# A hybrid mLSTM and gated DeltaNet layer on one core: a small tile is folded into another, and the mixers' tiles are padded

## The chip, the core and the metric

The kernel runs on one core of a Trainium2 chip. A core has five engines that work side by side: TensorE for matmuls (PE in the profile, with its weight loads as PEld), VectorE (DVE), ScalarE (ACT), GpSimd (POOL) and SyncE (SP), which here only issues transfers. They share an on-chip memory of 128 partitions (SBUF). A tile's place in it is a byte offset that is the same in all partitions, and "address" below means this offset. Matmuls accumulate in PSUM. The metric is the time of one execution on the device in microseconds (us). Before the change three runs gave a median of 2145.65 us, from 2143.23 to 2148.91.

## What is computed

One decoder block on 512 rows of width 2048, in float32. A single projection of the normalised input feeds an mLSTM branch with 8 heads and a gated DeltaNet branch with 16 heads; both go through one output projection and are merged with gates. Cut to what matters:

```python
u = rmsnorm(x, norm_w)                        # 512 x 2048
proj = u @ w_in                               # 2048 x 20528 columns
(ml_q, ml_k, ml_v, ml_o, ml_z, ml_i, ml_f,
 dn_qkv, dn_z, dn_b, dn_a, gate_a, gate_b) = split(proj)
h_a = mlstm_chunkwise(ml_q, ml_k, ml_v, softcap(ml_i), log_sigmoid(softcap(ml_f)))
h_a = rmsnorm_per_head(h_a) * ml_norm_w * sigmoid(ml_o) * silu(ml_z)
dq, dk, dv = split(silu(causal_conv(dn_qkv)))
g = -exp(a_log) * softplus(dn_a + dt_bias)    # log decay
h_b = gated_delta_chunkwise(l2norm(dq), l2norm(dk), dv, sigmoid(dn_b), g)
h_b = rmsnorm_per_head(h_b) * dn_norm_w * silu(dn_z)
y = sigmoid(gate_a) * (h_a @ w_out[:2048]) + sigmoid(gate_b) * (h_b @ w_out[2048:])
out = rmsnorm(x + y, final_norm_w)
```

## The kernel before

**The split of numbers.** A float32 weight is split in two pieces, `wh` (by ScalarE, `split_hi`, L146) and `wl` (the rest, by VectorE, `split_lo`, L149), and so are the activations, `uh` and `ul`. Each product is three matmuls: high by high, high by low, low by high. The matmuls' operands of 512 columns stream past a 128x128 block that was loaded before.

**The stages, in time.** First a front block, to 113.55 us: the normalisation, the transposes of the input, the first projections (`proj_cm`, L279) and the gates (`gates`, L460). Then the *seven-product stage* on `w_in`, to 1199.75 us. It computes two column blocks of 512 at a time with seven products of blocks in place of eight (`seven_stage`, L554). Its 14 pairs are listed in `SEVEN` (L52); each pair has 16 quads (8 of kind A, 8 of kind B), a quad of kind A has four products and one of kind B three, and a product (`product`, L646) is two rows of three matmuls, L652 to L654. That makes 14 x 56 x 6 matmuls, all of 512 columns. Then the *mixers*, which alternate the remaining projections (L272 to L274, L290 and L292) with the small matmuls of the two recurrences (`dn_back`, L1195, `dn_chain`, L1254, and the mLSTM heads behind them), among them groups of 128 and of 257 columns. Behind them come wide blocks on `w_out` (L1598 to L1600), the same seven-product function on `w_out` to about 2092 us, a last block and a short tail.

**Pieces in the seven-product stage.** For each quad SyncE loads three blocks of weights into a tile `wr3`. VectorE forms sums of them (`first_sums`, L590; the pair of sums is the tile `t13`). `split` (L581) then makes the pieces: *narrow* ones of 512 columns from the pool `wp` (tags `wh`, `wl`), and *wide* ones that hold two operands of 512 columns, from the stage's pool (tags `w2h`, `w2l`; each has two buffers of 4096 bytes). In a quad of kind A the products use the pieces in the order narrow, narrow, wide, wide; in kind B wide, wide, narrow. The order at a block's end (L675) puts the last two quads' narrow products together. In the profile a wide and a narrow low piece are both called `wl`.

**Where the tiles stand.** A pool places its tiles one behind the other in the order of their first use. The pool `sbp` (L422) of the first seven-product stage holds the tiles below; `turns` is declared 16 columns wide and one is used: +1 in the first 64 partitions, -1 in the others. `decay` (L888) uses it as a scale, beside a bias column of `pgam` with the negated decays, for heads `n` that are odd; so in `pgam`, with its 16 columns per chunk, the even columns are never read.

| tile | bytes | start |
|---|---|---|
| `w2h` | 2 x 4096 | 74752 |
| `pgam` | 256 | 82944 |
| `turns` | 64 | 83200 |
| `wr3` | 3 x 6144 | 83264 |
| `t13` | 4096 | 101696 |
| `w2l` | 2 x 4096 | 105792 |

The other operands of this stage's matmuls, the narrow pieces, `uh`, `ul`, `suh`, `sul`, `s4h` and `s4l`, start at multiples of 512. The final seven-product stage has a pool of its own (`sb2`) without `pgam` and `turns`; there `w2l` stands at 103424 and 107520.

**What sets the order.** TensorE's order is that of the code. On the other engines a scheduler orders instructions by readiness and priority: `high_priority` and `urgent(level)` (L225) lift an instruction, and `behind` (L152) puts it right behind the newest split. The mixers' generators are advanced by `tick` (L239) between groups of matmuls, so their small matmuls stand in fixed places among the projections.

Of the kernel before, what the change touches and what calls it, by code (L numbers as in the profile page):

```python
# [8 lines left out]
F32 = mybir.dt.float32  # L9
# [6 lines left out]
P = 128  # L16
S = 512
NC = S // P
D = 2048
KT = D // P  # L20
NB = 256
# [39 lines left out]
def hybrid_body(  # L61
# [18 lines left out]
    V, A, G, T = nc.vector, nc.scalar, nc.gpsimd, nc.tensor  # L80
# [144 lines left out]
    def urgent(level=1):  # L225
        return tc.high_priority(offset=level * PRIO)
# [195 lines left out]
    sbp = sbs.enter_context(tc.tile_pool(name="sbp", bufs=1))  # L422
# [31 lines left out]
    beta = cp.tile([P, NC, DNH], F32, tag="beta", name="beta")  # L454

    pgam = sbp.tile([P, NC, DNH], F32, tag="pgam", name="pgam")
    turns = sbp.tile([P, 16], F32, tag="turns", name="turns")[:, 0:1]
    for a, sign in ((0, 1.0), (64, -1.0)):
        G.memset(turns[a:a + 64], sign)
    def gates():  # L460
        rows = [sbp.tile([P, 3, S], F32, tag="wr3", name="grow", bufs=3) for _ in range(3)]

# [12 lines left out]
        tb = sml[:, 0, :, 0:16]  # L475
# [70 lines left out]
        A.activation(negeg, pc[:, :, 16:32], AF.Exp)  # L546
        V.tensor_copy(pgam[64:P], pc[64:P, :, 16:32])
        V.tensor_scalar(out=pgam[0:64], in0=pc[0:64, :, 16:32], scalar1=-1.0, scalar2=None, op0=ALU.mult)
        V.tensor_scalar(out=ngam, in0=pc[:, :, 16:32], scalar1=-1.0, scalar2=None, op0=ALU.mult)
        V.tensor_scalar(out=negeg, in0=negeg, scalar1=-1.0, scalar2=None, op0=ALU.mult)  # L550
        V.tensor_copy(acol, pc[:, :, 0:8])
# [447 lines left out]
    wk = wks.enter_context(tc.tile_pool(name="wkp", bufs=2))  # L999
    wkb = wkbs.enter_context(tc.tile_pool(name="wkb", bufs=2, side="right"))  # L1000
# [1 line left out]
    NYP = 2  # L1002
    yps = []
    for i in range(NYP):
        t = wkb.tile([P, S + 3], F32, tag=f"yp{i}", name=f"yp{i}", bufs=1)
        G.memset(t[:, 0:3], 0.0)
        yps.append(t)
    tb = wk.tile([P, 2 * NC, P], F32, tag="tb", name="tb", bufs=1)
    G.memset(tb, 0.0)
    ta = wk.tile([64, 2 * NC, 64], F32, tag="ta", name="ta", bufs=1)  # L1010
# [163 lines left out]
    def dn_front_q(hs, kq, u):  # L1174
        for j in range(2):
            pk = psw.tile([P, NC, P], F32, tag="wk", name="pqk")
            for c in range(NC):
                tsl = slice(c * P, (c + 1) * P)
                T.matmul(pk[:, c, :], kq[j][:, 0, tsl], kq[j][:, 1, tsl], start=True, stop=True)  # L1179
            dm, eg, ge = u["dm"][j]  # L1180
            with urgent():
                V.tensor_tensor(out=u["aq"][j][:, :, 1, :], in0=pk, in1=dm, op=ALU.mult)
            qt = kq[j][:, 1, :].rearrange("p (c t) -> p c t", t=P)
            G.tensor_tensor(out=qt, in0=qt, in1=eg, op=ALU.mult)
            u["qt"].append(qt)
            yield 1
        yield 9
        qe = wk.tile([P, 2, NC], F32, tag="qe", name="qe")
        with behind("A"):
            for j in range(2):  # L1190
                token_norms(u["qn"][j], qe[:, j, :])
        V.tensor_scalar(out=qe, in0=qe, scalar1=EPS, scalar2=EPS * P, op0=ALU.add, op1=ALU.mult)
        u["qe"] = qe

    def dn_back(hs, kq, u):  # L1195

        tn, tt = u["tn"], u["tt"]
        G2 = [(j * NC + c, u["aq"][j][:, c, 0, :]) for j in range(2) for c in range(NC)]
        for b in range(4):
            bs = slice(b * BS, (b + 1) * BS)  # L1200
            G.tensor_copy(tb[bs, :, bs], tt[bs])
        for b in range(2):
            bs = slice(b * BS, (b + 1) * BS)
            G.tensor_copy(ta[bs, :, bs], tn[bs])
        p1 = psw.tile([P, 2 * NC, BS], F32, tag="wk", name="p1")
        for g, a in G2:
            for q in range(2):
                a0, a1 = slice(64 * q, 64 * q + 32), slice(64 * q + 32, 64 * q + 64)
                T.matmul(p1[a1, g, :], a[a0, a1], tn[a0, g, :], start=True, stop=True)
        s1 = wk.tile([P, 2 * NC, BS], F32, tag="s3", name="s1", bufs=1)  # L1210
        for q in range(2):
            a1 = slice(64 * q + 32, 64 * q + 64)
            with urgent():
                A.mul(s1[a1], p1[a1], -1.0)
        for j in range(2):
            vn = u["vs"][j]
            with behind("V"):
                V.tensor_tensor(out=vn, in0=vn, in1=bc(u["nk"][:, j, :], P), op=ALU.mult)
        yield 2
        p2 = psw.tile([P, 2, 2 * NC, BS], F32, tag="wk", name="p2")  # L1220
        for g, a in G2:
            for q in range(2):
                a0, a1 = slice(64 * q, 64 * q + 32), slice(64 * q + 32, 64 * q + 64)
                T.matmul(p2[a0, 0, g, :], s1[a1, g, :], tt[a1, g, :], start=True, stop=True)
            T.matmul(p2[32:64, 1, g, :], tt[32:64, g, :], s1[32:64, g, :], start=True, stop=True)
        with urgent(2):
            V.tensor_copy(ta[32:64, :, 0:32], p2[32:64, 1])
        for q in range(2):
            a0, a1 = slice(64 * q, 64 * q + 32), slice(64 * q + 32, 64 * q + 64)
            with urgent():  # L1230
                A.copy(tb[a0, :, a1], p2[a0, 0])
        yield 3
        p3 = psw.tile([P, NC, 64], F32, tag="wk", name="p3")
        for c in range(NC):
            T.matmul(p3[64:128, c, :], G2[c][1][0:64, 64:128], ta[:, c, :], start=True, stop=True)
            T.matmul(p3[0:64, c, :], G2[NC + c][1][64:128, 0:64], tb[64:128, NC + c, 64:128], start=True, stop=True)
        s3 = wk.tile([P, NC, 64], F32, tag="s3", name="s3", bufs=1)
        with urgent():
            A.mul(s3[64:128], p3[64:128], -1.0)
            V.tensor_tensor(out=s3[0:64], in0=p3[0:64], in1=u["cs"][0:64, 1, :].unsqueeze(2).to_broadcast([64, NC, 64]),  # L1240
                            op=ALU.mult)
        yield 3
        p4 = psw.tile([P, NC, 64], F32, tag="wk", name="p4")
        for c in range(NC):
            T.matmul(p4[0:64, c, :], s3[64:128, c, :], tb[64:128, c, 64:128], start=True, stop=True)
            T.matmul(p4[64:128, c, :], ta[:, NC + c, :], s3[0:64, c, :], start=True, stop=True)
        with urgent():
            V.tensor_copy(tb[0:64, 0:NC, 64:128], p4[0:64])
            A.mul(tb[0:64, NC:2 * NC, 64:128], p4[64:128], -1.0)
        soon = hs[0] == 2 * UNITS[-1]  # L1250
        start(dn_chain(0, hs, kq, u, soon), 3 - soon)
        start(dn_chain(1, hs, kq, u, soon), 4 - soon)

    def dn_chain(j, hs, kq, u, soon):  # L1254
# [2 lines left out]
        vn = u["vs"][j]  # L1257

        po = pso.tile([P, NC, P], F32, tag="o", name="po")
        ssq = wk.tile([P, NC], F32, tag="ssq", name="ssq")  # L1260
        st = None
        for c in range(NC):
            tsl = slice(c * P, (c + 1) * P)
# [98 lines left out]
    def ml_head(h):  # L1362
# [25 lines left out]
        qi = qT.rearrange("p (c t) -> p c t", t=P)  # L1388
        G.tensor_tensor(out=qi, in0=qi, in1=iwb, op=ALU.mult)
        yield 3  # L1390
        v1 = wkb.tile([P, NC, NB + 16], F32, tag="mv1", name="v1", bufs=1)[:, :, 0:NB + 1]
        G.memset(v1[:, :, NB:NB + 1], 1.0)
        nc.sync.dma_start(v1[:, :, 0:NB], v_d[:, :, h * NB:(h + 1) * NB].rearrange("c p n -> p c n"))
        yield 6
# [2 lines left out]
                A.mul(kw[:, c, :], kw[:, c, :], we[:, c:c + 1])  # L1397
        yield 2

        sq = wk.tile([P, NC], F32, tag="sq", name="sq")  # L1400
        c1 = None
        for c in range(NC):
            pn = psw.tile([P, NB + 1], F32, tag="wk", name="pnum")
            T.matmul(pn, w[:, c, :], v1[:, c, :], start=True, stop=(c1 is None))
            if c1 is not None:
                T.matmul(pn, qi[:, c, :], c1, start=False, stop=True)
            yield 1
            if c < NC - 1:
                pcs = psw.tile([P, NB + 1], F32, tag="wk", name="pcs")
                T.matmul(pcs, kw[:, c, :], v1[:, c, :], start=True, stop=True)  # L1410
                cn = wkb.tile([P, NB + 16], F32, tag="c1", name="c1")[:, 0:NB + 1]
                with urgent():
                    if c1 is None:
                        V.tensor_copy(cn, pcs)
                    else:
                        V.scalar_tensor_tensor(out=cn, in0=c1, scalar=de[:, c:c + 1], in1=pcs,
                                               op0=ALU.mult, op1=ALU.add)
                c1 = cn
            with urgent():
                A.copy(v1[:, c, :], pn)  # L1420
            jk = wk.tile([P, NB], F32, tag="jk", name="mjk", bufs=1)
            A.activation(jk, v1[:, c, 0:NB], AF.Square, accum_out=sq[:, c:c + 1])
            if c == NC - 2:
                g = [wk.tile([P, NC, P], F32, tag="g", name="mg", bufs=2) for _ in range(2)]
                for i in range(2):
                    col = h * NB + i * P
                    nc.sync.dma_start(g[i], g_d[:, :, col:col + P].rearrange("c p n -> p c n"))
            yield 3
# [547 lines left out]
```

## Time and profile before

| | |
|---|---|
| median of 3 runs | 2145.65 us (2143.23 to 2148.91) |
| the profiled execution's own time | 2146.57 us |
| its span in the trace | 2144.8 us |
| front block | 0 to 113.55 us |
| seven-product stage on `w_in` | 113.55 to 1199.75 us |
| mixers and wide blocks | 1199.75 to 1937 us |
| seven-product stage on `w_out` | 1937 to 2092 us |
| last block and tail | 2092 to 2144.8 us |

The profile is of one execution. The span runs from its first to its last instruction; 1.8 us of the execution's time lie around it. Matmuls are pipelined: one takes 0.39 us or so from its start to the end that the profile models, and the next one starts before that, so the busy time of TensorE says little about how close they follow. The distance from one start to the next is read from the view of instructions in order of time (the timeline), or as the length of a stretch divided by the number of matmuls in it. Rows of the groups of instructions read: line, engine, operation, written tile <- read tiles, shapes, xcount | busy us, mean ns | idle us ahead of them and what ended it.

### The profile page before, as it was taken

To read this page: it belongs to the slowest core of one execution; us is meant where nothing else is said; L and a number is where in the kernel's file an instruction comes from. 1 tells how busy PE (TensorE), PEld (TensorE's weight loads), DVE (VectorE), ACT (ScalarE), POOL (GpSimd) and SP (SyncE) were. 2 spreads that over 40 slices of the span, in tenths; PEclk is the share of its full clock that TensorE was granted. 3 is DMA by queue.
4 is the path that set the end of the run, shared out by engine and by line. 5 is a ranking of instruction groups with operands and counts; after the bars stand their busy time and mean duration, and the time that the engine had idled before them with its cause. 6 is when DMAs were issued, how large, how long until landed. Compare 5 with 4: busy or idle time off the path is not lost.

```text
span 2144.8 us, 32556 instructions
## 1 busy us (share of the span) xinstructions
PE 2125.8 (99%) x10507; PEld 1744.9 (81%) x10507; DVE 1746.6 (81%) x3026; ACT 1086.4 (51%) x2103; POOL 473.2 (22%) x697
## 2 busy tenths in 40 slices
PE   9999999999999999999999999999999999999998
PEld 7888888888888888888888888888888888887886
DVE  5988898898888887888887587797788779569887
ACT  4445555555554455454454444544554465335445
POOL 1211011001014001210000233434434344132211
PEclk9999999999999999999999999999999999999999
DMA  6476777777787878787879876768777868778886
GB/s 177 140 221 216 252 220 229 235 244 243 242 261 239 279 245 270 227 248 239 244 225 345 265 206 170 203 177 216 206 185 213 210 160 240 197 215 287 256 293 230
DMA packets 476389, 491.75 MB, mean 229 GB/s; under 512 B 192485, under 2 KB 304842, under 8 KB 476090
## 3 DMA queue, kind: packets, MB, share of 16 engines
q1 hardware_dynamic: 379354, 363.96, 57.9%
q0 software_dynamic: 25216, 73.16, 10.8%
q10 hardware_dynamic: 71648, 52.55, 7.5%
q8 instruction: 82, 1.34, 0.3%
q14 instruction: 89, 0.73, 0.1%
HBM read 376.71 MB, written 117.02 MB: 230 GB/s over the span
## 4 chain that ended last, share of the span: by engine, by line
PE 92%; DMA 4%; DVE 2%; ACT 1%; issue 1%; POOL 1%; SPq 0%; ACTq 0%; POOLq 0%; DVEq 0%
PE ps L653 19%; PE ps L652 19%; PE ps L654 19%; PE pj L292 13%; PE pj L290 7%; PE py L1598 2%; PE py L1600 2%; PE py L1599 2%; DMA wr<-in_w_out_dram 1%; DMA h_d<-to 1%; PE pj L272 1%; PE pj L273 1%; PE pj L274 1%; PE pqk L1179 1%; PE pw L1276 1%
## 5 line engine op out<-in xcount | busy, mean ns | idle before, releaser
L150 DVE TENSOR_TENSOR wl<-wr,wh 128x512 fp32r<-128x512 f32 (+1 forms) x506 | 430.1, 851 | 164.3 <-ACT wh L147 146.6
L147 ACT CAST wh<-wr 128x512 fp32r<-128x512 f32 (+1 forms) x506 | 366.7, 726 | 385.3 <-PE pj L292 146.2
L653 PE MATMUL ps<-wl,uh 128*128 128x512 f32 x800 | 313.8, 392 | 0.1
L652 PE MATMUL ps<-wh,uh 128*128 128x512 f32 x800 | 313.2, 392 | 0.0
L654 PE MATMUL ps<-wh,ul 128*128 128x512 f32 x800 | 312.8, 391 | 0.0
L290 PE MATMUL pj<-uh,wh 128*128 128x512 f32 x672 | 283.9, 422 | 0.5 <-ACT yp L1030 0.5
L147 ACT CAST wh<-t 128x1024 fp32r<-128x1024 f32 x128 | 134.3, 1049 | 290.3 <-PE ps L654 207.6
L653 PE MATMUL ps<-wl,suh 128*128 128x512 f32 x672 | 265.0, 394 | 0.0
L652 PE MATMUL ps<-wh,suh 128*128 128x512 f32 x672 | 264.1, 393 | 0.0
L292 PE MATMUL pj<-uh,wl 128*128 128x512 f32 x672 | 263.2, 392 | 0.6 <-DVE wl L150 0.6
L654 PE MATMUL ps<-wh,sul 128*128 128x512 f32 x672 | 263.5, 392 | 0.0
L292 PE MATMUL pj<-ul,wh 128*128 128x512 f32 x672 | 262.8, 391 | 0.0
L147 ACT CAST wh<-ts 128x512 fp32r<-128x512 f32 x256 | 157.7, 616 | 160.6 <-DVE ts L612 134.5
L607 POOL DMA_DIRECT2D t_d<-ts x112 | 61.8, 552 | 780.1 <-DVE ts L594 765.0
L150 DVE TENSOR_TENSOR wl<-t,wh 128x1024 fp32r<-128x1024 f32 x128 | 157.4, 1230 | 77.5 <-ACT wh L147 77.5
L150 DVE TENSOR_TENSOR wl<-ts,wh 128x512 fp32r<-128x512 f32 x256 | 175.5, 686 | 18.6 <-ACT wh L147 17.2
L652 PEld LDWEIGHTS ps<-wh,uh 128*128 128x128 f32 x800 | 150.2, 188 | 35.0
L653 PEld LDWEIGHTS ps<-wl,uh 128*128 128x128 f32 x800 | 150.1, 188 | 34.4 <-DVE wl L150 0.8
L654 PEld LDWEIGHTS ps<-wh,ul 128*128 128x128 f32 x800 | 150.3, 188 | 33.3
L593 DVE TENSOR_TENSOR t<-wr 128x1024 f32<-128x1024 f32 x128 | 158.7, 1240 | 8.7 <-DMA wr<-in_w_in_dram 4.8
L652 PEld LDWEIGHTS ps<-wh,suh 128*128 128x128 f32 x672 | 126.1, 188 | 29.3 <-ACT qk L407 0.4
L653 PEld LDWEIGHTS ps<-wl,suh 128*128 128x128 f32 x672 | 126.0, 188 | 29.1 <-DVE wl L150 0.7
(372 smaller groups left out, 4094.5 us busy)
## 6 DMA issues: line engine op xcount, KB each, us to landing
wr<-in_w_in_dram SPq DMA_DIRECT2D x728, 256.0 KB, 4.1
wr<-in_w_out_dram SPq DMA_DIRECT2D x138, 256.0 KB, 5.2
t_d<-ts POOLq DMA_DIRECT2D x112, 256.0 KB, 4.6
wr<-t_d SPq DMA_DIRECT2D x112, 256.0 KB, 4.7
wr<-in_w_in_dram SPq DMA_DIRECT2D x48, 128.0 KB, 2.3
to<-rows_d SPq DMA_DIRECT2D x24, 256.0 KB, 5.3
dm_d<-to ACTq DMA_DIRECT2D x24, 256.0 KB, 3.6
us_d<-uhi ACTq DMA_DIRECT2D x16, 256.0 KB, 2.9
```

The source lines that it names most:

```text
L147: newest["A"] = A.copy(hi, src).ins
L150: newest["V"] = V.tensor_tensor(out=lo, in0=src, in1=hi.bitcast(F32), op=ALU.subtract).ins
L290: T.matmul(ps[j], hi[:, k, wsl], uh[:, kt, :], start=(kt == 0), stop=False)
L292: T.matmul(ps[j], w[:, k, wsl], x_[:, kt, :], start=False, stop=(kt == KT - 1 and w is lo))
L593: V.tensor_tensor(out=t13, in0=r[:, 1:3, :], in1=r[:, 0:2, :], op=ALU.subtract)
L607: queue.dma_start(t2_d[b % 2, i], ts[:, 0, :])
L652: T.matmul(ps[t], ah, hi, start=(g == "A" and i == 0), stop=False, skip_group_check=True)
L653: T.matmul(ps[t], ah, lo, start=False, stop=False, skip_group_check=True)
L654: T.matmul(ps[t], al, hi, start=False, stop=(i == KH - 1), skip_group_check=True)
L1598: T.matmul(ps[c], uh[:, kt, tsl], hi, start=(kt == ks[0]), stop=False)
L1599: T.matmul(ps[c], uh[:, kt, tsl], lo, start=False, stop=False)
L1600: T.matmul(ps[c], ul[:, kt, tsl], hi, start=False, stop=(kt == ks[-1]))
```

## The change

The tile `turns` goes; its values move into column 0 of `pgam`, which is even and so free. The two memsets that write them move from GpSimd, at the beginning, to VectorE in `gates`, behind the instructions that write `pgam`. In the mixers' pools the widths of `yp`, `qe`, `ssq`, `sq`, `v1` and `c1` are padded, so that all tiles there start at multiples of 128 bytes; what is computed in them is the same. In `dn_back` the copies into `tb` and `ta` on GpSimd get a higher priority.

```diff
     pgam = sbp.tile([P, NC, DNH], F32, tag="pgam", name="pgam")
-    turns = sbp.tile([P, 16], F32, tag="turns", name="turns")[:, 0:1]
-    for a, sign in ((0, 1.0), (64, -1.0)):
-        G.memset(turns[a:a + 64], sign)
+    turns = pgam[:, 0, 0:1]
     def gates():
...
         V.tensor_copy(pgam[64:P], pc[64:P, :, 16:32])
         V.tensor_scalar(out=pgam[0:64], in0=pc[0:64, :, 16:32], scalar1=-1.0, scalar2=None, op0=ALU.mult)
+        for a, sign in ((0, 1.0), (64, -1.0)):
+            V.memset(turns[a:a + 64], sign)
...
-        t = wkb.tile([P, S + 3], F32, tag=f"yp{i}", name=f"yp{i}", bufs=1)
+        t = wkb.tile([P, S + 32], F32, tag=f"yp{i}", name=f"yp{i}", bufs=1)[:, 0:S + 3]
...
-        qe = wk.tile([P, 2, NC], F32, tag="qe", name="qe")
+        qe = wk.tile([P, 2, 8], F32, tag="qe", name="qe")[:, :, 0:NC]
...
-            G.tensor_copy(tb[bs, :, bs], tt[bs])
+            with urgent(2):
+                G.tensor_copy(tb[bs, :, bs], tt[bs])
...
-            G.tensor_copy(ta[bs, :, bs], tn[bs])
+            with urgent(2):
+                G.tensor_copy(ta[bs, :, bs], tn[bs])
...
-        ssq = wk.tile([P, NC], F32, tag="ssq", name="ssq")
+        ssq = wk.tile([P, 16], F32, tag="ssq", name="ssq")[:, 0:NC]
...
-        v1 = wkb.tile([P, NC, NB + 16], F32, tag="mv1", name="v1", bufs=1)[:, :, 0:NB + 1]
+        v1 = wkb.tile([P, NC, NB + 32], F32, tag="mv1", name="v1", bufs=1)[:, :, 0:NB + 1]
...
-        sq = wk.tile([P, NC], F32, tag="sq", name="sq")
+        sq = wk.tile([P, 16], F32, tag="sq", name="sq")[:, 0:NC]
...
-                cn = wkb.tile([P, NB + 16], F32, tag="c1", name="c1")[:, 0:NB + 1]
+                cn = wkb.tile([P, NB + 32], F32, tag="c1", name="c1")[:, 0:NB + 1]
```

In the first stage's pool, `wr3` then starts at 83200, `t13` at 101632 and the two buffers of `w2l` at 105728 and 109824; `w2h`, the pieces in `wp` and the final stage's pool stay. In the mixers, `kq` of odd units goes from 76224 to 76288, `v1` from 152064 in steps of 1088 bytes to 151680 in steps of 1152, and the two buffers of `c1` from 161152 and 162240 to 161024 and 162176.

The instructions of TensorE stand in the same order as before, row for row. On VectorE, these rows stand where the gates' last columns leave PSUM, ahead of the seven-product stage; `pc` is the PSUM tile with the transposed gates, `X` is a sum of `u_sums`. Before:

```order
L547 COPY pgam<-pc 64x64
L548 TENSOR_SCALAR pgam<-pc 64x64
L549 TENSOR_SCALAR ngam<-pc 128x64
L550 TENSOR_SCALAR negeg<-negeg 128x64
L551 COPY acol<-pc 128x32
L552 COPY emcol<-pc 128x32
L438 TENSOR_TENSOR X<-X 128x256
L440 TENSOR_TENSOR X<-X 128x256
L439 TENSOR_TENSOR X<-X 128x256
```

And on VectorE now, at the same place:

```order
L545 COPY pgam<-pc 64x64
L546 TENSOR_SCALAR pgam<-pc 64x64
L549 TENSOR_SCALAR ngam<-pc 128x64
L550 TENSOR_SCALAR negeg<-negeg 128x64
L551 COPY acol<-pc 128x32
L552 COPY emcol<-pc 128x32
L438 TENSOR_TENSOR X<-X 128x256
L440 TENSOR_TENSOR X<-X 128x256
L548 MEMSET pgam 64x1 x2
L439 TENSOR_TENSOR X<-X 128x256
```

The two memsets stand behind all that leaves PSUM there and between two sums of `u_sums`.

On GpSimd, in the mixers, these rows belong to the fifth unit: `tb` and `ta` are the copies of the change, `rsd` and `gz` scale the previous unit's result, `dm` and `ke` belong to this unit's decays and keys, `sm` and `mg` to an mLSTM head. Before:

```order
L1310 TENSOR_TENSOR rsd<-ssq,mhalf 128x4
L1201 COPY tb<-tt 32x8x32 x3
L1311 TENSOR_TENSOR gz<-gz,rsd 128x512
L1201 COPY tb<-tt 32x8x32
L1310 TENSOR_TENSOR rsd<-ssq,mhalf 128x4
L1311 TENSOR_TENSOR gz<-gz,rsd 128x512
L1204 COPY ta<-tn 32x8x32 x2
L1136 TENSOR_TENSOR nk<-nk,half 128x8
L1134 TENSOR_TENSOR dm<-dm,cs 128x512 x2
L1435 TENSOR_TENSOR sm<-sm,mhalf 128x4
L1160 TENSOR_TENSOR ke<-ke,dm 128x512
L1135 MEMSET dm 64x4x64
```

And on GpSimd now, in the same unit:

```order
L1312 TENSOR_TENSOR rsd<-ssq,mhalf 128x4
L1202 COPY tb<-tt 32x8x32 x4
L1313 TENSOR_TENSOR gz<-gz,rsd 128x512
L1312 TENSOR_TENSOR rsd<-ssq,mhalf 128x4
L1313 TENSOR_TENSOR gz<-gz,rsd 128x512
L1206 COPY ta<-tn 32x8x32 x2
L1136 TENSOR_TENSOR nk<-nk,half 128x8
L1437 TENSOR_TENSOR sm<-sm,mhalf 128x4
L1134 TENSOR_TENSOR dm<-dm,cs 128x512 x2
L1440 TENSOR_TENSOR mg<-mg,sm 128x512 x2
L1160 TENSOR_TENSOR ke<-ke,dm 128x512
L1135 MEMSET dm 64x4x64
```

The fourth copy into `tb` no longer stands behind a `gz`; `sm` comes ahead of `dm`, and `mg` ahead of `ke`. In the other seven units GpSimd's order is as it was.

## The prediction

> **What bounds the kernel now.** I read the page from the top: first the busy times, then the chain of work that ended last.
>
> ```profile
> span 2144.8 us, 32556 instructions
> PE 2125.8 (99%) x10507; PEld 1744.9 (81%) x10507; DVE 1746.6 (81%) x3026; ACT 1086.4 (51%) x2103; POOL 473.2 (22%) x697
> PEclk9999999999999999999999999999999999999999
> PE 92%; DMA 4%; DVE 2%; ACT 1%; issue 1%; POOL 1%; SPq 0%; ACTq 0%; POOLq 0%; DVEq 0%
> ```
>
> TensorE is busy 2125.8 of 2144.8 us and makes 92% of the chain, at full clock in every slice. Only 19 us of the span are free of a matmul. So a change counts if it alters how fast the matmuls follow one another, or if it makes TensorE wait where it does not wait now. Next comes the view by stretches, for TensorE alone: start and end, length, busy time with the number of instructions that overlap the stretch, clock, DMA share, GB/s.
>
> ```profile
> 113.55:1199.75 1086.20, 1086.20 (x4706) 1.00 0.78 248
> 1199.75:1937.00 737.25, 731.95 (x4418) 1.00 0.76 204
> 2035.00:2135.00 100.00, 100.00 (x443) 1.00 0.77 263
> ```
>
> The first row is the seven-product stage on `w_in`, half of the kernel. TensorE never stops in it: busy 1086.20 of 1086.20 us. It holds 14 blocks of 56 products of 6 matmuls, 4704 (the row counts two neighbours that reach over its edges). All have 512 columns, so one starts every 1086.20 / 4704 = **230.91 ns**. The last row lies in the end of the kernel, where the same function runs on `w_out` and then the last block follows, with 512 columns in each matmul too: (100 + 0.39) / 443 = **226.6 ns**, 0.39 us being what one matmul reaches over the edge. The clock is 1.00 in both. "Busy" hides this difference, for overlapping matmuls leave no idle time whether they follow at 227 or at 231 ns. I therefore went to the timeline, around the end of one block of the first stage: start, duration, line, operands.
>
> ```profile
> 576.65 0.39 PE L652 MATMUL ps<-wh,uh 128*128 128x512 f32 x1
> ...
> 582.09 0.39 PE L652 MATMUL ps<-wh,suh 128*128 128x512 f32 x1
> 582.32 0.40 PE L653 MATMUL ps<-wl,suh 128*128 128x512 f32 x1
> 582.56 0.40 PE L654 MATMUL ps<-wh,sul 128*128 128x512 f32 x1
> 582.80 0.39 PE L652 MATMUL ps<-wh,suh 128*128 128x512 f32 x1
> 583.02 0.39 PE L653 MATMUL ps<-wl,suh 128*128 128x512 f32 x1
> 583.25 0.39 PE L654 MATMUL ps<-wh,sul 128*128 128x512 f32 x1
> 583.48 0.40 PE L652 MATMUL ps<-wh,suh 128*128 128x512 f32 x1
> 583.71 0.40 PE L653 MATMUL ps<-wl,suh 128*128 128x512 f32 x1
> ...
> 585.56 0.39 PE L652 MATMUL ps<-wh,suh 128*128 128x512 f32 x1
> ```
>
> From 576.65 to 582.09 stand 24 matmuls, four products in a row whose pieces are all narrow: 5.44 / 24 = 226.7 ns. At 582.09 the first product with a wide piece begins. Its first `wl` starts at 582.32, the next start comes 0.24 us later and the one after it 0.24 us, and from there to 585.56 the 15 starts take 3.47 us, 231.3 ns each. So the slow pace is not the stage's, it comes with the wide pieces. By the sizes of the tiles, the wide low pieces (`w2l`) stand at bytes 105792 and 109888, which is 64 past a multiple of 128; every other operand that streams or is loaded as weights in this stage starts at a multiple of 512 bytes. In the final stage the wide low pieces start at 103424 and 107520, both multiples of 512, and there the same line with the same kind of piece runs evenly:
>
> ```profile
> 2046.20 0.39 PE L652 MATMUL ps<-wh,tu 128*128 128x512 f32 x1
> 2046.43 0.39 PE L653 MATMUL ps<-wl,tu 128*128 128x512 f32 x1
> ...
> 2048.24 0.39 PE L652 MATMUL ps<-wh,tu 128*128 128x512 f32 x1
> ```
>
> Nine starts in 2.04 us, 226.7 ns. I read this as: a streamed operand of 512 columns that starts 64 bytes off makes its own matmul and those that follow a little late, until some narrow products have gone by.
>
> **The change part by part.**
>
> *`turns` out of the pool.* 64 bytes ahead of `wr3`, `t13` and `w2l` go, so `w2l` stands at 105728 and 109824: multiples of 128, though 256 past a multiple of 512. PE's order of instructions and waits is the same, row for row. What this is worth, if 128 bytes are what counts, is the stage at the even pace: 4704 x 226.67 ns = 1066.3 us in place of 1086.2, that is 19.9 us less. I take 0.3 us off, for a wait in a seven stage that the list of waits shows and that no address mends:
>
> ```profile
> PE ps L653 <- DVE wl L150: 0.3, 1, 0.3
> ```
>
> So **-19.6 us**. From both sides: if the 64 bytes are not the cause it is 0; if 256 past 512 were the worst class it is a loss, priced below. I take the full value, because the class that the trace shows clean (multiples of 512) and the new one differ in nothing that the block's end tells apart, while the old one is the only one in the stage off a multiple of 128. No row shows a stream at 256 past 512; that is the weakest joint of this prediction.
>
> The faster matmuls need their pieces 1.8% sooner. The same view by stretches with all engines (PE, PEld, DVE, ACT, POOL, clock, DMA share, GB/s) for the stage and for the final one:
>
> ```profile
> 150.00:1150.00 1000.00, 1000.00 (x4334) 813.05 (x4333) 855.46 (x1100) 532.90 (x829) 122.51 (x195) 1.00 0.78 245
> 2040.00:2090.00 50.00, 50.00 (x223) 41.38 (x222) 43.01 (x59) 22.84 (x32) 8.97 (x13) 1.00 0.89 295
> ```
>
> VectorE would rise from 86% to 855.46 / 982 = 87% busy, and the DMA share from 0.78 to about 0.79. In the final stage VectorE at 86% and DMA at 0.89 and 295 GB/s serve the even pace without a stop. So cover remains. The page's slices show VectorE at 9 tenths or more twice early in the stage; if TensorE waited there for the whole gain, 2 x 53.6 us x 1.8% = 1.9 us would be lost, and I keep that as the upper side of this term.
>
> *The signs written by VectorE.* Two memsets of 64x1 leave POOL and two join VectorE's row in `gates()`:
>
> ```profile
> L459 POOL MEMSET turns<- x2: 94/110/127, 46.9 to 47.1; 64x1 f32 x2
> L551 DVE COPY acol<-pc 128x32 f32<-128x32 f32 x1 | 0.2, 175 | 0.0
> L303 DVE MEMSET warm<- 128x128 f32 x1 | 0.2, 165 | 0.8 <-PEq L1963 0.8
> ```
>
> On VectorE a memset of 128x128 takes 165 ns and a copy of 128x32 175 ns, so the two cost at most 0.35 us of VectorE at 106 us, within the row of `u_sums`. TensorE runs the last matmuls of the front block above them without a stop; without that cover they would cost their 0.35 us. Nothing less than 0 is possible, as POOL's two were early and nobody waited for them. I take 0. The activations at L905, which read the signs, read `pgam` beside them anyway, so they already wait for VectorE's row there.
>
> *The mixers' tiles padded, and POOL's copies made urgent.* The middle row of the first table of stretches bounds this: TensorE is busy 731.95 of 737.25 us there. What alignment could do is read by operation (count, busy, mean ns, idle ahead):
>
> ```profile
> L290 PE MATMUL pj<-uh,wh 128*128 128x512 f32 x544 | 232.6, 428 | 0.5 <-ACT yp L1030 0.5
> L292 PE MATMUL pj<-uh,wl 128*128 128x512 f32 x544 | 212.9, 391 | 0.0
> L292 PE MATMUL pj<-ul,wh 128*128 128x512 f32 x544 | 212.7, 391 | 0.0
> L1102 PE MATMUL pk<-kq 128*128 128x128 f32 x128 | 16.8, 274 | 0.0
> L1179 PE MATMUL pqk<-kq 128*128 128x128 f32 x128 | 17.0, 276 | 0.0
> ```
>
> The long streams of the mixers are `uh` and `ul`, which do not move. Their means are 389 ns where all is even; 391 says that a matmul soon after an interruption by a small group starts late. All of that is 2 ns x 1088 plus the like of `proj_half`, about 2.6 us, and it is the most that better places of `kq`, `v1` and `c1` could give back here. The 428 of L290 is the first matmul after a group, (428 - 389) x 544 = 21 us, the price of changing from one kind of matmul to another; no padding removes it, though a new class of address might shift it by a tenth, 2 us either way. So this part lies between -5 and +5 us, and I take **0**, since `kq` and the 257-column groups stand on both kinds of address already and the small ones differ by 2 ns of 275. The urgent copies:
>
> ```profile
> L1201 POOL COPY tb<-tt 32x256 f32<-32x256 f32 x32 | 15.8, 493 | 11.2 <-DMA tt<-xd 8.0 <-PE pj L274 2.1
> L1311 POOL TENSOR_TENSOR gz<-gz,rsd 128x512 f32<-128x512 f32 x14 | 15.5, 1109 | 0.7
> L1438 POOL TENSOR_TENSOR mg<-mg,sm 128x512 f32<-128x512 f32 x16 | 18.2, 1156 | 0.4
> PE p L1235 <- POOL dm L1134: 1.6, 1, 1.6
> ```
>
> In one unit of eight, the four copies now all stand ahead of a `gz` product (1.1 us) on POOL, and there `sm` comes ahead of the two `dm`, and the two `mg` ahead of the first `ke`. TensorE waits for POOL once in these stages, 1.6 us, so at best that goes. At worst the matmuls that read `ke` (L1283) wait for what now stands ahead of it, two `mg` and the small `sm`, about 2 x 1.16 + 1 = 3.3 us by the rows of their kind, once. I take 0 and keep both ends.
>
> **Sum**, against the profiled execution's own 2146.57 us (span 2144.8 and 1.8 around it): 2146.57 - 19.6 + 0 + 0 + 0 = 2127.0. The median of the runs before, 2145.65, lies 0.9 below the profiled one, so as a median 2126.
>
> **The rivals.**
>
> *The pace has another cause, and the change does nothing: 2146.* The wide pieces are also those that VectorE writes in long instructions, and the first stage has them 14 blocks long; traffic could be what slows it. For it speaks only that no row isolates the address. Against it: at 295 GB/s with VectorE as busy the final stage runs evenly, and the first stage itself does so for 24 matmuls at a block's end with the same traffic. The address alone may also not matter to a stream, each of which reads 512 consecutive values wherever it starts; then the four narrow products would be quick for their own reasons. 2146.57 less the 0.9 is 2145.7. [...]
>
> *Half a cure: 2136.* The unit that counts may be larger than 128 bytes; then a start 256 past 512 still disturbs, only less often. No row gives the share, so I put it in the middle of both ends: 19.6 / 2 = 9.8 us, 2126 + 10 = 2136.
>
> *The new place is worse: 2157, slower.* If distance from the nearest multiple of 512 is what counts, the old starts (320 past) lay 192 bytes away and the new ones lie 256 away, the furthest possible. A dear product of today is one with `s4h`, whose piece is wide:
>
> ```profile
> 575.25 0.40 PE L652 MATMUL ps<-wh,s4h 128*128 128x512 f32 x1
> ```
>
> It runs from there to 576.65, 1.40 us for 6, against a mean of 1086.20 / 784 = 1.385. If the new class made every product so dear, 784 x 0.0146 = 11.4 us would come on top: 2145.7 + 11.4 = 2157. It decides as soon as the excess per matmul exceeds today's 4.2 ns. Against it: the disturbance starts at a `wl` that is off by 64, not at the `w2h` streams which start at 0.
>
> **How the numbers follow.** The even pace 0.77 (2126, its own range 2121 to 2131), half a cure 0.08, no change 0.10, worse 0.05. The range 2121 to 2139 takes in the first two with the mixers' bounds and the spread of the runs before (2143 to 2149, 3 us either way), and leaves 0.15 and a little of the edges out. About 0.3%, 6.4 us, is what a measurement of this kernel can tell from no change; below 2139.2 lie the first two cases but for a sliver, so faster 0.84, within 0.11, slower 0.05.
>
> **What would show it.** The stage that begins at 113.55 should end near 1180, not 1199.75; a stretch of 1000 us in it should hold some 4415 matmuls, not 4334; the mean of L653 on `wl,suh` there should fall to 389 ns, and the timeline should show 0.22 to 0.23 between starts at the wide products too. From the stage's end to the span's end it should stay at 2144.8 - 1199.75 = 945 us within 5. It is wrong if the starts behind a wide `wl` still come 0.24 apart, or if TensorE now shows idle time in the stage with VectorE or a DMA as releaser.

## The result, and the profile after

The changed kernel took 2130.82 us (median of 4 runs, 2130.33 to 2133.33) beside 2147.22 us of the kernel before in the same comparison (2143.23 to 2148.91): a ratio of 0.9929, with a 95% interval of 0.9911 to 0.9946. The forecast was 2126, in a range of 2121 to 2139. A later, longer comparison gave 0.991 (0.9894 to 0.9927). The page of the changed kernel, its profiled execution (2133.33 us):

```profile
span 2131.6 us, 32554 instructions
PE 2108.2 (99%) x10507; PEld 1744.5 (82%) x10507; DVE 1745.0 (82%) x3028; ACT 1087.0 (51%) x2103; POOL 472.8 (22%) x695
PE 84%; DMA 4%; DVE 3%; issue 1%; ACT 1%; POOL 1%; SPq 0%; DVEq 0%; POOLq 0%; ACTq 0%
```

TensorE lost 17.6 us of busy time and is still the bound. By stretches (TensorE's busy time and count, clock, DMA share, GB/s), the first seven-product stage and what follows up to the final one:

```profile
113.80:1185.20 1071.40, 1068.15 (x4706) 1.00 0.78 251
1185.20:1922.00 736.80, 732.62 (x4419) 1.00 0.76 204
```

The same 4706 matmuls as in the row of before, in 1071.4 us in place of 1086.2; but now TensorE stands still for 3.25 us of them, where before it never stopped. The mixers kept their length, 736.8 us against 737.25. The timeline at a quad's two wide products, and the end of the stage (start, duration, line, operands):

```profile
604.65 0.39 PE L652 MATMUL ps<-wh,suh 128*128 128x512 f32 x1
604.88 0.39 PE L653 MATMUL ps<-wl,suh 128*128 128x512 f32 x1
605.10 0.39 PE L654 MATMUL ps<-wh,sul 128*128 128x512 f32 x1
605.33 0.39 PE L652 MATMUL ps<-wh,suh 128*128 128x512 f32 x1
605.56 0.39 PE L653 MATMUL ps<-wl,suh 128*128 128x512 f32 x1
605.78 0.39 PE L654 MATMUL ps<-wh,sul 128*128 128x512 f32 x1
...
606.92 0.39 PE L653 MATMUL ps<-wl,suh 128*128 128x512 f32 x1
...
1185.17 0.39 PE L290 MATMUL pj<-uh,wh 128*128 128x512 f32 x1
```

Ten starts in 2.27 us, 227 ns, through the first wide `wl`: the 0.24 us behind it are gone. To count this over the whole stage I take from the trace the distance of each start to the next, leave out those over 260 ns (there TensorE waits for something, or starts again behind a wait), and add up what lies over 226.67 ns; below this sum is called the *excess*. It was 19.35 us before and is 0.25 us now, so the pace gave 19.1 us. The distances over 260 ns came to 0.6 us beyond the pace before and to 4.9 us now. Hence the stage: 19.1 - 4.3 = 14.8 us shorter. The front block is 0.3 us and all behind the stage 1.4 us longer, and 14.8 - 0.3 - 1.4 = 13.1; the spans differ by 2144.8 - 2131.6 = 13.2 us, the same but for rounding. The final seven-product stage, whose wide pieces stood well before too, serves as a control: the like sum over its 672 matmuls is 0.2 to 0.3 us in every profile of this document.

### The profile page after: what moved, and what is told of

Read it like the earlier page. It is cut to its first block, busy times and chain, and to the rows that moved or that the text cites. A ratio compares the mean times of both kernels' runs of the same rounds, so it can differ in the third digit from the quotient of the medians.

```text
span 2131.6 us, 32554 instructions
## 1 busy us (share of the span) xinstructions
PE 2108.2 (99%) x10507; PEld 1744.5 (82%) x10507; DVE 1745.0 (82%) x3028; ACT 1087.0 (51%) x2103; POOL 472.8 (22%) x695
## 3 DMA queue, kind: packets, MB, share of 16 engines
q8 instruction: 82, 1.34, 0.3%
## 4 chain that ended last, share of the span: by engine, by line
PE 84%; DMA 4%; DVE 3%; issue 1%; ACT 1%; POOL 1%; SPq 0%; DVEq 0%; POOLq 0%; ACTq 0%
PE ps L653 18%; PE ps L654 18%; PE ps L652 18%; PE pj L292 11%; PE pj L290 6%; PE py L1600 2%; PE py L1601 2%; PE py L1602 2%; DVE wl L150 1%; PE pj L272 1%; PE pj L274 1%; PE pj L273 1%; DMA wr<-in_w_out_dram 1%; PE pqk L1179 1%; PE pw L1278 1%
## 5 line engine op out<-in xcount | busy, mean ns | idle before, releaser
L593 DVE TENSOR_TENSOR t<-wr 128x1024 f32<-128x1024 f32 x128 | 157.3, 1229 | 14.8 <-DMA wr<-in_w_in_dram 8.7
L292 PEld LDWEIGHTS pj<-uh,wl 128*128 128x128 f32 x672 | 126.4, 188 | 27.7 <-DVE wl L150 1.0
```

What stands on the lines that cost most here:

```text
L292: T.matmul(ps[j], w[:, k, wsl], x_[:, kt, :], start=False, stop=(kt == KT - 1 and w is lo))
L593: V.tensor_tensor(out=t13, in0=r[:, 1:3, :], in1=r[:, 0:2, :], op=ALU.subtract)
```

## The experiments

Where nothing else is said, a kernel is the changed one with the edit shown. TensorE's order of instructions is the same in all of them. "Excess" is the sum described above, over the 4704 matmuls of the first stage.

**The signs alone.** The kernel before with the first and second piece of the diff and nothing else.

> The kernel before with one edit: the signs in column 0 of pgam, nothing else. Theory (the start of the wide low pieces makes the gain): all of it is here, about 2131 us as with the whole change, the stretch 150 to 1150 us holds some 4410 matmuls, the mean of L653 on wl,suh is 389 ns. Rival (the padded mixers or the urgent copies make part of it): 2135 us or more, with 4410 matmuls in the stretch all the same.

```profile
150.00:1150.00 1000.00, 999.80 (x4409) 1.00 0.79 250
L653 PE MATMUL ps<-wl,suh 128*128 128x512 f32 x634 | 246.8, 389 | 0.1
```

2131.27 us against 2149.5 (ratio 0.9914, 0.989 to 0.9939), excess 0.27 us. The whole gain that can be told is in the 64 bytes.

**The rest alone.** The changed kernel with `turns` a tile again:

```diff
-    turns = pgam[:, 0, 0:1]
+    turns = sbp.tile([P, 16], F32, tag="turns", name="turns")[:, 0:1]
+    for a, sign in ((0, 1.0), (64, -1.0)):
+        G.memset(turns[a:a + 64], sign)
...
-        for a, sign in ((0, 1.0), (64, -1.0)):
-            V.memset(turns[a:a + 64], sign)
```

> The changed kernel with the tile turns and its GpSimd memsets put back, so only the padded mixers and the urgent copies remain. Theory: the pace of the first seven-product stage is as before (4334 matmuls in 150 to 1150 us, L653 on wl,suh 394 ns) and the time is that of before within 0.1%, 2145 to 2149 us. Rival: 2 us or more of the gain stay here, under 2144 us.

2149.71 us against 2149.5 (1.0003, 0.999 to 1.0016); the excess is 19.36 us, that of before to 0.01. The padding and the urgent copies are worth nothing that a comparison can tell. The like sum behind the 2496 matmuls of 512 columns between the two seven-product stages, distances up to 260 ns, even went from 5.3 or 5.4 us (with the signs alone, and before) to 6.0 us (both kernels with the padding). What their longer distances hold differs more between two executions of the changed kernel (33.1 and 36.4 us) than between these kernels.

**Only the wide low pieces moved back.**

```diff
         sml = sbp.tile([P, 2, NO], F32, tag="t13", name="sml").rearrange("p a n -> p (a n)")[:, 0:240 * NC]
+        pad = sbp.tile([P, 16], F32, tag="pad", name="pad")
+        G.memset(pad, 0.0)
```

> The changed kernel with a tile of 64 bytes ahead of the wide low pieces alone: w2l back at 105792 and 109888, while wr3 and t13 keep their new places at multiples of 128. Theory (only what TensorE streams counts): back to 2147 us, 4334 matmuls in the stretch, VectorE's means as they are. Rival (the place of wr3 or t13, which VectorE, ScalarE and the DMAs use, counts): it stays near 2131 us, or lands between.

```profile
150.00:1150.00 1000.00, 999.68 (x4331) 1.00 0.78 244
```

2149.42 us against 2149.5 (1.0004, 0.9992 to 1.0015), excess 19.38 us. `wr3` and `t13` stand where the changed kernel has them and do not matter; `w2l` does.

**Which offsets cost.** The same pad made 8, 24 and 32 columns wide (32, 96 and 128 bytes; the first is shown), and, for 16 bytes, the pieces 4 columns inside a longer tile in place of a pad:

```diff
+        pad = sbp.tile([P, 8], F32, tag="pad", name="pad")
+        G.memset(pad, 0.0)
```

```diff
-                hi, lo = (sbp.tile([P, 2, NO], F32R, tag=f"w2{n}", name=f"w{n}", bufs=2) for n in "hl")
+                hi = sbp.tile([P, 2, NO], F32R, tag="w2h", name="wh", bufs=2)
+                off = 4 if k0 == 0 else 0
+                lo = sbp.tile([P, 2 * NO + 8 * off], F32R, tag="w2l", name="wl", bufs=2)[:, off:off + 2 * NO]
+                lo = lo.rearrange("p (a n) -> p a n", n=NO)
```

> The changed kernel with a tile of 32 bytes ahead of the wide low pieces: w2l at 32 past a multiple of 128. Theory (any start off a multiple of 128 costs about the same): 2147 us, some 4334 matmuls in the stretch. Rivals: a unit of 32 bytes counts, then it stays at 2131 us; or the loss goes with the part that lies over the edge, then 32 bytes cost about half of what 64 bytes do, 2139 us, some 4372 matmuls.

> The changed kernel with the wide low pieces of the first stage in tiles 128 bytes longer, used from 16 bytes behind their start: the stream starts 16 past a multiple of 128. So far 64 past costs 4.1 ns a matmul over 226.67 and 32 past 2.9 ns. Theory A (the loss grows with the offset up to 64): about 1.5 ns, some 4382 matmuls in 150 to 1150 us. [...]

> The changed kernel with 96 bytes ahead of the wide low pieces: 96 past a multiple of 128. Theory A (the shorter of the two parts at an edge counts): like 32 past, 2.9 ns over 226.67, some 4356 matmuls in the stretch. Theory B (the loss goes on growing with the offset): 5 ns or more, 4318 or fewer.

> The changed kernel with 128 bytes ahead of the wide low pieces: at 0 past a multiple of 128, but 384 past one of 512 where the changed kernel has 256. Theory (the unit is 128 bytes): clean, some 4410 matmuls in the stretch, as with the changed kernel. Rival (the class within 512 or 256 bytes counts and 256 happens to be a good one): slower than 226.67 ns by 1 ns or more, fewer than 4390.

| `w2l` past a multiple of 256 bytes | kernel | excess, us | matmuls in 150 to 1150 us |
|---|---|---|---|
| 0 | the changed kernel | 0.25 | 4394 |
| 16 in one buffer, 144 in the other | 16 bytes further | 17.4 | 4323 |
| 32 | 32 further | 13.6 | 4356 |
| 64 | 64 further | 19.4 | 4331 |
| 96 | 96 further | 18.7 | 4334 |
| 128 | 128 further | 6.2 | 4375 |

(The counts also hold the waits, which differ between executions; the excess does not.) With 32 bytes further the comparison gave 2144.56 us, 0.9979 (0.9966 to 0.9992); 16, 96 and 128 bytes further are single runs. Of the theories and rivals of this row only the last rival held: the class within 256 or 512 bytes counts, and the place of the changed kernel happens to be a good one. 16 bytes further are not free (17.4 us), the loss is not in proportion to the offset (13.6 us at 32 bytes, 19.4 at 64, 18.7 at 96), and a multiple of 128 is not enough: at 128 past a multiple of 256 a third of the loss is back (6.2 of 19.4 us).

```profile
150.00:1150.00 1000.00, 997.73 (x4375) 1.00 0.79 248
L655 PE MATMUL ps<-wl,suh 128*128 128x512 f32 x626 | 246.2, 393 | 1.9 <-DVE wl L150 1.9
L656 PE MATMUL ps<-wh,sul 128*128 128x512 f32 x626 | 243.1, 388 | 0.0
```

This is the kernel with 128 bytes further; the edit shifted its line numbers by two. The mean of `wl` (L655) is up at 393 ns. Over the stage 891 of the 896 starts right behind a wide `wl` come 234 or 235 ns after it; of the other 3808 distances only 36 are between 230 and 260 ns.

**The wide high pieces moved.**

```diff
     X = sbp.tile([P, 2, 2, NO], F32, tag="X", name="X")
+    hpad = sbp.tile([P, 16], F32, tag="hpad", name="hpad")
+    G.memset(hpad, 0.0)
...
         sml = sbp.tile([P, 2, NO], F32, tag="t13", name="sml").rearrange("p a n -> p (a n)")[:, 0:240 * NC]
+        pad = sbp.tile([P, 16], F32, tag="pad", name="pad")
+        G.memset(pad, 0.0)
```

> The changed kernel with 64 bytes ahead of the wide high pieces (w2h at 64 past a multiple of 128) and 64 bytes ahead of the wide low ones, so that these stay at a multiple of 128. The high pieces are streamed by two of the three matmuls, the low by one. Theory (each shifted stream adds its own price): twice the loss of the kernel before, 8.2 ns a matmul, the stage 39 us longer, about 2169 us. Rival (a disturbance lasts some ten matmuls and does not add up, so the stage just stays disturbed): the loss of before or little over it, 2147 to 2155 us.

2150.93 us against 2149.17 (1.0013, 1.0001 to 1.0024), excess 21.5 us. The low pieces stand at 128 past 256 here and cost 6.2 us by themselves, so the high ones, two streams in three, add 15 us, not 39. In this kernel the prices do not add up: its time is in the rival's range. The high pieces alone were not moved.

**The weight loads moved.** `suh` is never streamed; here it starts 64 past a multiple of 256, and all streams stay.

```diff
-    suh, sul = (sap.tile([P, KH, 3, HP], F32R, tag=f"su{n}", name=f"su{n}") for n in "hl")
+    suh = sap.tile([P, KH * 3 * HP + 48], F32R, tag="suh", name="suh")[:, 0:KH * 3 * HP]
+    suh = suh.rearrange("p (k a n) -> p k a n", a=3, n=HP)
+    sul = sap.tile([P, KH, 3, HP], F32R, tag="sul", name="sul")
```

> The changed kernel with suh, which is loaded as weights for two of three matmuls in three of seven products and is streamed by none, moved to 64 past a multiple of 256; all streams stay. Theory (only the streamed operand counts): 4410 matmuls in 150 to 1150 us, excess under 0.5 us. Rival (the start of a weight load counts as well): mean distance above 227.5 ns, under 4398 matmuls.

```profile
150.00:1150.00 1000.00, 1000.00 (x4348) 1.00 0.78 246
L654 PE MATMUL ps<-wh,suh 128*128 128x512 f32 x619 | 246.3, 398 | 0.0
L656 PE MATMUL ps<-wh,sul 128*128 128x512 f32 x618 | 245.1, 397 | 0.0
L655 PE MATMUL ps<-wl,s4h 128*128 128x512 f32 x208 | 80.9, 389 | 0.0
```

Excess 15.9 us, one run of 2145.84 us. So my theory of the stream alone fell: the start of what is loaded as weights counts too. The products on `s4h`, which didn't move, keep 389 ns. The timeline with the weight loads, where a product on `uh` ends and one on `suh` begins:

```profile
602.93 0.39 PE L656 MATMUL ps<-wh,ul 128*128 128x512 f32 x1
602.93 0.19 PEld L654 LDWEIGHTS ps<-wh,suh 128*128 128x128 f32 x1
603.15 0.40 PE L654 MATMUL ps<-wh,suh 128*128 128x512 f32 x1
603.15 0.19 PEld L655 LDWEIGHTS ps<-wl,suh 128*128 128x128 f32 x1
603.39 0.39 PE L655 MATMUL ps<-wl,suh 128*128 128x512 f32 x1
603.39 0.19 PEld L656 LDWEIGHTS ps<-wh,sul 128*128 128x128 f32 x1
603.62 0.40 PE L656 MATMUL ps<-wh,sul 128*128 128x512 f32 x1
603.62 0.19 PEld L654 LDWEIGHTS ps<-wh,suh 128*128 128x128 f32 x1
```

The load for the next matmul (0.19 us here) runs beside the stream of the present one (0.39 or 0.40 us). Over the whole stage the distance is 236 ns in the mean where `suh` is loaded beside `wh,suh`, 235 where it is loaded beside `wh,sul`, and 229 where `sul` is loaded, beside `wl,suh`. But the first load of `suh`, beside `wh,ul`, costs nothing: 226 ns.

**Everything moved.** 64 bytes at the very beginning of the left side of SBUF, and 64 bytes less behind `ul` on the right: every tile of the kernel stands 64 bytes further.

```diff
+    first = cp.tile([P, 16], F32, tag="first", name="first")
+    G.memset(first, 0.0)
     ident = cp.tile([P, P], F32, tag="ident", name="ident")
...
-    ul = up.tile([P, KT * S + 120], F32R, tag="ul", name="ul")
+    ul = up.tile([P, KT * S + 104], F32R, tag="ul", name="ul")
```

> The changed kernel with every tile of the kernel, on both sides of SBUF, 64 bytes further: 64 bytes at the very beginning of the left side, 64 fewer of the padding behind ul on the right. Streams and weight loads keep their distances from one another and all start at 64 past a multiple of 256. Theory (the address itself counts): every product is disturbed, in all stages, so at least the 21 us of the shifted wide pieces in the first stage and as much per matmul in the final one, 2153 us or more, 4326 matmuls or fewer in 150 to 1150 us. Rival (what counts is how a stream stands to the weight load that runs beside it): nothing changes, 2131 us, some 4400 matmuls.

```profile
150.00:1150.00 1000.00, 997.73 (x4400) 1.00 0.80 250
L655 PE MATMUL ps<-wl,suh 128*128 128x512 f32 x633 | 246.7, 390 | 1.9 <-DVE wl L152 1.9
```

2132.78 us against 2149.03 (0.9919, 0.99 to 0.9938), excess 0.08 us: as clean as the changed kernel, with every operand 64 bytes past a multiple of 256. `w2l` starts at 105792 again, the very address at which it cost 19 us. The rival held in that nothing changed. **So 64 past a multiple of 256 is not bad by itself: in these runs the pace is even where the streamed and loaded operands stand alike within 256 bytes, and uneven where one of them is moved against the others.**

**The changed kernel again, and its waits.** The second of these has one edit, the queue of the writes `t_d<-ts`:

```diff
-    lead, seven = seven_stage(sbp, (suh, sul), (s4h, s4l), X, t2_d, w_in, 0, SEVEN, SINK, begin_mixers, G, ahead)
+    lead, seven = seven_stage(sbp, (suh, sul), (s4h, s4l), X, t2_d, w_in, 0, SEVEN, SINK, begin_mixers, nc.scalar, ahead)
```

> The changed kernel once more, for its time over more runs and a second profile. Theory (the gain is the even pace, 19.1 us by the excess of before, and the waits that came beside it are the execution's own): 2129 to 2132 us against 2147 to 2150 of before, a ratio near 0.991; PE's waits in the first seven-product stage between 0.6 and 7 us, as in the other profiles, at the same place near 522 us. Rival (the faster pace makes new waits): those waits 4 us or more again, ratio 0.993 or above.

> The changed kernel with the writes t_d<-ts of the first stage issued by ScalarE in place of GpSimd. Theory (the stop near 522 us comes from the write of ts on GpSimd's queue landing late, VectorE waits for it to reuse ts): no start over 400 ns late there, PE's waits in the stage about 1 us, 2 us less than the changed kernel beside it. Rival (all writes land late there, whichever queue): the stop stays, and the time is within 1 us of the changed kernel or above it, as ScalarE's queue holds the stage's other writes.

The changed kernel took 2133.57 us against 2149.8 (0.991, 0.9894 to 0.9927; its runs reach from 2126.56 to 2137.63), and the second profile has 5.6 us of distances over 260 ns in the stage: the ratio is that of the theory, the time is 1.6 us above its range, and the waits fit both. With the writes issued by ScalarE it took 2132.57 (0.9919, 0.9906 to 0.9933), with 3.5 us of such distances; the stop near 522 us shrank to one distance of 1.34 us but did not go. Neither theory of that run holds whole, and its time is not told apart from the changed kernel's. In the changed kernel's first profile TensorE's timeline shows the largest stop:

```profile
522.48 0.39 PE L654 MATMUL ps<-wh,sul 128*128 128x512 f32 x1
523.46 0.49 PE L652 MATMUL ps<-wh,suh 128*128 128x512 f32 x1 [0.60 <-ACT wh L147]
525.81 0.50 PE L653 MATMUL ps<-wl,suh 128*128 128x512 f32 x1 [1.85 <-DVE wl L150]
```

VectorE, one step back, waited for the write of `ts` to be done, in order to use its buffer again:

```profile
522.07 0.69 DVE L594 TENSOR_TENSOR ts<-wr,t 128x512 f32<-128x512 f32 x1 [3.63 <-DMA t_d<-ts]
```

And on GpSimd, which issues those writes, another step back:

```profile
508.28 0.54 POOL L607 DMA_DIRECT2D t_d<-ts  x1 [4.67 <-DVE ts L594]
515.66 1.03 POOL L899 TENSOR_SCALAR_AFFINE_SELECT to<-to 128x512 f32<-128x512 f32 x1 [6.84 <-DMA to<-rows_d]
516.64 0.56 POOL L607 DMA_DIRECT2D t_d<-ts  x1
```

The write at 516.64 stands behind a mask of `decay` (L899) that waits for its own load of rows until 515.66; 8.4 us lie between the two issues. Before the change the same mask stood ahead of the same write, the two issues lay 6.9 us apart, and VectorE waited 0.79 us behind them. But the late issue alone does not make the stop. The kernel with the signs alone has the same 8.4 us (the write before went out at 508.07) and only a short wait:

```profile
516.45 0.56 POOL L607 DMA_DIRECT2D t_d<-ts  x1
519.05 0.69 DVE L594 TENSOR_TENSOR ts<-wr,t 128x512 f32<-128x512 f32 x1 [0.80 <-DMA t_d<-ts]
```

There VectorE goes on 2.6 us after the issue, here 5.4 us after it, and it is this landing that makes the stop; why the write took longer is not known. Is the stop a price of the faster pace? The old pace has it too: the kernel with the rest alone shows the most, 7.0 us of distances over 260 ns beyond the pace in its stage. But (the kernel with 128 bytes aside) of the eight profiles with a slow pace six have 1.6 us or less, and of the five with an even one, the one with the writes on ScalarE among them, four have 3.5 us or more (1.6 to 5.6). The means are 2.3 and 3.8 us, so the even pace seems to meet it more often, by 1.5 us or so; with one profile of most kernels that is not settled. To issue the mask later was not tried.

## Why the prediction was right, point by point

- **What bounds.** Right: TensorE's pace in the first stage gave the gain, and no other part gave any that can be told.
- **The pace.** Forecast -19.6 us; the excess fell by 19.1 us. By the whole time the first comparison gives 16 us (12 to 19), and the longer one 0.9% of 2149.8, 19 us (16 to 23). The mean of `wl,suh` came to 389 ns as foretold. Half a cure, no change and a worse place did not come.
- **Its reason was wrong in two places.** The prediction let "a streamed operand of 512 columns that starts 64 bytes off" be the cause, and took 128 bytes for the unit. The kernel with `suh` moved and the one with everything moved show that it is the difference between operands, loads included, and the one with 128 bytes further that 128 is not the unit; 256 fits all runs. The new place happened to be 256 past a multiple of 512, where all other operands stand at 0. That was luck: the joint that the prediction called its weakest held by the 256, not by the 128. The rival of half a cure had this much right, that the unit is larger than 128 bytes. A kernel whose piece had gone from 64 to 128 past would have won two thirds, by the one run with 128 bytes further.
- **The cover.** The prediction kept up to 1.9 us for waits in VectorE's fullest slices. The waits of the profiled execution were 4.3 us above those of before. Most of them, 2.9 us, lie at one place near 522 us that is not among these slices, behind a late write of `ts`. The term was too small for this execution; how much of it is the change's stays open, as said above. With the 1.7 us ahead of the stage and behind it, these waits are why the two profiled spans are 13.2 us apart and not 19.1. The prediction named idle time in the stage with VectorE as releaser as a sign of being wrong, and this sign came (1.85 us behind `wl`): it was wrong about the cover, not about the pace.
- **The memsets, the padding, the urgent copies.** Forecast 0 each; the kernel with the rest alone shows 1.0003 (0.999 to 1.0016) for the last two, and with the signs alone there is no loss to be seen beside the gain.

What stays open is which two operands have to stand alike. The old kernel moved a stream against streams and loads; the one with `suh` moved a load against loads and streams. A stream against the weight load that runs beside it would explain both with one mechanism. The trace with `suh` moved bears it out in part (236 and 235 ns against 229) and not whole, as the first load of `suh` behind `uh` came without delay. No run moved one against the other alone, and why 256 bytes matter is not shown.

## What to carry to other kernels

Where TensorE is busy without a gap, still measure the distance from start to start: 231 against 227 ns did not show in TensorE's busy share, 99% in both, and was worth 0.9%. Then look at the byte offsets of the streamed and the loaded operands within 256 bytes: a small tile ahead of large ones in a pool shifts them all, and here it was enough to keep them alike, at 0 or at 64 past a multiple of 256. The free column cost nothing that could be told, but check such a move with the pace of the matmuls and not with the multiple of 128 bytes by which it was chosen.

## What the runs showed that was not expected

- The kernel with every operand at 64 past a multiple of 256 runs like one with every operand of this stage at a multiple of it (excess 0.08 and 0.25 us), while 64 bytes between operands cost 16 us (`suh` moved) or 19 us (`w2l` moved) in the stage, and 128 bytes 6 us.
- At 64 bytes a disturbed matmul also delays those behind it: in the kernel before, the narrow products, none of whose operands is off, start every 229.6 ns in the mean, the wide ones every 231.7. At 128 bytes hardly any such delay shows (36 distances of 3808 between 230 and 260 ns, as said above). And shifted operands need not add up: all three streams off (the high by 64, the low by 128) cost hardly more than the low alone by 64 (21.5 against 19.4 us).
- A stop can cost more than its length. In the second profile of the changed kernel the stop near 522 us was followed by five distances of 0.43 us, with a granted clock of 0.69 from 526 to 530 us. Its timeline:

```profile
525.51 0.79 PE L653 MATMUL ps<-wl,suh 128*128 128x512 f32 x1 [1.85 <-DVE wl L150]
526.10 0.63 PE L654 MATMUL ps<-wh,sul 128*128 128x512 f32 x1
526.53 0.63 PE L652 MATMUL ps<-wh,suh 128*128 128x512 f32 x1
```

  and, by stretches of the same kernel (busy time and count of TensorE, clock, DMA share, GB/s):

```profile
523.00:526.00 3.00, 0.99 (x2) 0.84 0.45 176
526.00:530.00 4.00, 4.00 (x14) 0.69 0.54 138
```

  In the first profile a stop of about the same length had no such tail (0.34 and then 0.23 us from start to start behind it). Of the six profiles with a distance of 2.35 us near there, three have the tail (this one, the rest alone and 16 bytes further) and three have none.
